# Where a block's second norm is applied: gathering x1 instead of h2, and transposing with a scaled diagonal

## The chip, the cores and the metric

The kernel runs on one core of a Trainium2 chip. TensorE (PE in the profile, PEld for its weight loads), VectorE (DVE), ScalarE (ACT) and GpSimd (POOL) compute; SyncE (SP) issues most DMAs, and POOL the indirect ones. The metric is the device time of one launch in microseconds (us).

## The reference

One decoder block of 1024 tokens with 1024 features, all in float32. After two kinds of attention and an out-projection comes a mixture of 32 experts, of which each token uses two:

```python
x  = x + gate_mix * (mixed @ w_out)                       # x1 in the kernel
h2 = rmsnorm(x, g_ffn) * (1 + scale_ffn) + shift_ffn
group  = argmax(softmax(h2 @ w_group))                    # 4 groups of 8 experts
top_p, expert = top_k(softmax(h2 @ w_expert within group), 2)
weight = max(group softmax) * top_p / sum(top_p)
y[token] += weight * ((silu(h2 @ w_gate[e]) * (h2 @ w_up[e])) @ w_down[e])
out = rmsnorm(x + gate_ffn * y, g_final)
```

Scale, shift and gates come from a conditioning vector, one value per feature. So h2 of a token is x1 times one factor of the token (r2, the reciprocal root of its mean square), times one factor per feature (`affn`), plus one shift per feature.

## The kernel before

The program goes through projections, eight attention passes, an out-projection with routing, the experts, and a last norm. Instructions stand in program order on each engine; the order of what lies beside attention is written out in lists of units (`work`, `end_units`), which are taken a few at a time between the steps of a pass.

The weights of the experts come in 384 loads of 512 KB, twelve per expert (eight for gate and up, four for down), through one SP queue (`load_to`, L973). Each load goes into a slot of the pool `u`, which has 49 slots that all large tiles share: a slot is 128 partitions by 1028 floats (4112 bytes; 4128 from slot to slot in the compiled program), of which most tiles use 1024. Some 36 loads are issued ahead; from the 35th on they are queued behind the gather of expert 1 (`after`).

In the last attention pass and after it, each 128-token tile goes through units: `out_mm` makes x1 (L674); `norm2` squares it on ACT and stores it to `acc` in DRAM; `norm2r` makes r2 on POOL (L933 and the helper `rsqrt`, L177 to L193); `norm2b` makes h2 from x1 in place, a DVE multiply by r2 and a feature row (L940) and an addition of another feature row on POOL (L941; on DVE where `late`), and stores it to `h2d`; `route0` transposes x1, `logits` multiplies it by the router's matrix (the norm's feature factors are folded into that), `route1` picks group and experts in some twelve DVE steps, `exps` is on ACT, `route2` counts ranks, `lists` makes one list of token numbers per expert by a product of two one-hot matrices (L868, L869), and `route3` makes the weights (L876 to L882). Weights and expert numbers go in 16 bytes behind each row of `h2d`, so a row there has 4112 bytes. The last two tiles t and u are routed together, their DVE steps interleaved.

Then come a spread of the gate row (L626), 80 warm-up products (L268), the first gathers (`load_x`, an indirect DMA of up to 96 or 64 rows by POOL, L1226), and `places`, which sorts the experts from 4 on by size, so that their lists and weights are taken in that order (`perm`, `permi`, `lsP`).

The expert loop takes the steps of `order`: G is one of eight gate-and-up steps, X the transpose of the expert after the next (`xpose`, L1241, between the sixth and seventh G step of the expert before it), T transposes the activations, D is one of four down steps, Y weighs and adds to `acc` with an indirect DMA. `xpose` turns the gathered rows by eight TensorE transposes into one or two PSUM banks, copies these to SBUF on ACT (L1242), and makes the expert's weights `wt` from the 16 bytes (L1244, L1246).

Of the kernel before, what the change touches and what calls it, by code (L numbers as in the profile page):

```python
# [28 lines left out]
ROW = 1028  # L29
# [34 lines left out]
HS = 7  # L64
QS = "ASS"
# [4 lines left out]
RG = 1  # L70
# [32 lines left out]
def build(nc, tc, I, out, cap=CAP):  # L103
# [14 lines left out]
    QA, QH, QE = (E_[c] for c in QS)  # L118
# [16 lines left out]
    def slot(name, dt=F32):  # L135
        return up.tile([128, ROW], dt, name=name, tag="u")[:, :1024]

# [188 lines left out]
    rows = dp.tile([3, 1024], F32, name="rows")  # L326

    def ada_units():
        us = []
        st = {}  # L330

        def fetch(v, k):
            st[v, k] = ada(v, k)

        def red(v, k):
            ada_red(st[v, k], v, k)

# [21 lines left out]
        us.append(router)  # L359
        return us  # L360
# [383 lines left out]
    h2d = dp.tile([T, ROW], F32, name="h2d")  # L744
# [4 lines left out]
    perm = cp.tile([128, NE], F32, name="perm")  # L749
# [15 lines left out]
    def section(tt):  # L765

        if "room" not in R:
            R["room"] = slot("room")
        n = 320 * (TL.index(tt) % 3)
        return R["room"][:, n:n + 320]  # L770
# [21 lines left out]
    def route1(tt):  # L792
# [5 lines left out]
        V.scalar_tensor_tensor(zz[:, 0:36], lp, R2[tt], zc, op0=ALU.mult, op1=ALU.add)  # L798
# [40 lines left out]
    def route2(tt, before=()):  # L839
# [10 lines left out]
        j1, r["j"] = at[:, 256:256 + NE], at[:, 288:288 + NE]  # L850
# [13 lines left out]
    def lists(*tts):  # L864
        lp = bank(f"ls{tts[0]}", (cap, NE))
        ms = [(R[tt]["at"][c], R[tt][o]) for tt in tts for c, o in enumerate(("o1", "o2"))]
        for n, (a, o) in enumerate(ms):
            PE.matmul(lp, a, o, start=(n == 0), stop=(n == len(ms) - 1))  # L868
        V.tensor_add(ls if TL[-1] in tts else lacc, lacc, lp)  # L869

    def route3(tt):
# [10 lines left out]
        V.tensor_sub(ext[:, 2:3], ext[:, 0:1], ext[:, 1:2])  # L882
        QE.dma_start(h2d[tt * 128:tt * 128 + 128, 1024:ROW], ext[:, 1:5])
# [7 lines left out]
    def places():  # L891
# [13 lines left out]
        A.activation(lsT, c2[:32, 0:cap], AF.Copy)  # L905
# [13 lines left out]
    R2 = {}  # L919

    def norm2(tt):
        x1 = X1[tt]
        R[tt] = slot(f"x1T_{tt}")
        ss2 = R2[tt] = sp.tile([128, 2], F32, name=f"ss2_{tt}", tag="ss2")
# [3 lines left out]
        QA.dma_start(acc[tt * 128:tt * 128 + 128, :], x1)  # L928

    def norm2r(tt):  # L930
        ss2 = R2[tt]
        R2[tt] = sp.tile([128, 1], F32, name=f"r2_{tt}", tag="r2", bufs=3)
        (G if RG else V).tensor_add(ss2[:, 0:1], ss2[:, 0:1], ss2[:, 1:2])  # L933
        rsqrt(R2[tt], ss2[:, 0:1], 1, 1.0 / D, G if RG else V)
# [52 lines left out]
    def alloc_x(e):  # L987
        XE[e] = up.tile([128, ROW], F32, name=f"xe{e}", tag="u")
        G.memset(XE[e][:capof(e)], 0.0)

    def end_units():
# [3 lines left out]
        us = [p0(lambda: (load_bc(1, "a"), load_bc(2, "sh"), load_x1(TL[0], acc), load_x1(TL[1], acc)))]  # L995
# [9 lines left out]
        for n in range(KT + 1):  # L1005
# [216 lines left out]
    def load_x(e):  # L1222
        if e not in XE:
            alloc_x(e)
        xe = XE[e]
        g = G.indirect_dma_start(out=xe[:capof(e)], out_offset=None, in_=h2d[:],  # L1226
# [198 lines left out]
    with tc.If(rv > 0):  # L1425
# [15 lines left out]
        with tc.For_i(0, NE, 1) as e:  # L1441
# [6 lines left out]
            for tt in range(KT):  # L1448
                c = slice(tt * 128, tt * 128 + 128)
                x, xt, act, y, a = work2[tt % 2]  # L1450
                nc.sync.dma_start(x, h2d[c, 0:1024])
                for s in (0, 1):
                    tp = bank(f"oxp{tt}_{s}")
                    for i in range(4):
                        k = 4 * s + i
                        PE.transpose(tp[:, i * 128:(i + 1) * 128], x[:, k * 128:(k + 1) * 128], ident)
                    V.tensor_copy(xt[:, s * 512:(s + 1) * 512], tp)
# [109 lines left out]
```

## Time and profile before

| | us |
|---|---|
| median of three runs (lowest, highest) | 1358.26 (1356.75, 1359.79) |
| the profiled execution | 1359.39 |
| its span | 1357.5 |
| TensorE busy | 1173.9 (86%) |
| VectorE busy | 740.4 (55%) |
| ScalarE busy | 457.9 (34%) |
| GpSimd busy | 287.8 (21%) |

The times in the rows are those of the profiled execution, counted from the start of its span. A busy share over the whole span is a mean over stages with different limits, so the table is only the start: the rows below are cut by stage. A row of the timeline has its start, its duration, engine, line, operation, what is written from what, shapes, and in brackets how long the engine had been idle before and what released it. An fp32 product counts two records there.

### The profile page before, as it was taken

How to read it: one execution, taken by the hardware profiler on the slowest of the kernel's cores; microseconds unless marked ns; L12 is line 12 of the kernel's file. 1: busy time of each engine (PE TensorE's matmuls, PEld its weight loads, DVE VectorE, ACT ScalarE, POOL GpSimd, SP SyncE). 2: the span in 40 equal slices, each digit the busy share in tenths (PEclk: the TensorE clock that was granted, in tenths of full speed). 3: DMA queues.
4: the chain of work that ended last, by engine and by line, in shares of the span. 5: the costliest groups of instructions: out<-in, count | busy, mean ns of one | idle time of the engine just before them, and what ended most of it. 6: DMA issues, size and time to landing. Idle time of an engine off the chain costs nothing. (4 is left out here: it accounts for less than half of the span.)

```text
span 1357.5 us, 19273 instructions
## 1 busy us (share of the span) xinstructions
PE 1173.9 (86%) x6843; PEld 688.0 (51%) x6843; DVE 740.4 (55%) x1378; ACT 457.9 (34%) x913; POOL 287.8 (21%) x341
## 2 busy tenths in 40 slices
PE   4699989999999998898876999999998888888960
PEld 3487778778867885676655533333332222222310
DVE  6958773774697768788967233333332223322224
ACT  5246553655555445334322121111211111111112
POOL 3600100120000102325334121211221111111203
PEclk9799999999999999899988899999999999999995
DMA  9322432462101011457666889999999999999984
GB/s 355 152 78 93 162 133 94 144 53 69 32 16 47 17 63 40 151 183 264 217 217 233 282 314 374 355 360 363 365 371 369 362 368 370 373 373 378 347 279 190
DMA packets 92904, 305.65 MB, mean 225 GB/s; under 512 B 15681, under 2 KB 18113, under 8 KB 92802
## 3 DMA queue, kind: packets, MB, share of 16 engines
q1 hardware_dynamic: 85298, 283.08, 58.3%
q0 software_dynamic: 6352, 17.08, 5.4%
q10 hardware_dynamic: 1152, 4.19, 0.8%
q8 instruction: 56, 0.92, 0.3%
q14 instruction: 46, 0.38, 0.1%
HBM read 279.39 MB, written 29.65 MB: 228 GB/s over the span
## 5 line engine op out<-in xcount | busy, mean ns | idle before, releaser
L1255 PE MATMUL gu<-ew,xs 128*64 128x512 f32 x1024 | 249.8, 611 | 8.3 <-DMA ew<-we 8.0
L1313 DVE TENSOR_TENSOR ys<-y,bc_gate 64x512 f32<-64x512 f32 x64 | 44.0, 688 | 260.1 <-PE y L1262 109.4
L1255 PE MATMUL y<-ew,at 128*64 128x512 f32 x512 | 128.4, 620 | 25.6 <-DMA ew<-we 23.9
L1255 PEld LDWEIGHTS gu<-ew,xs 128*64 128x64 f32 x1024 | 63.7, 137 | 142.7 <-issue 88.5
L1328 POOL DMA_INDIRECT acc<-ys,lsP x27 | 38.9, 1440 | 361.7 <-DVE ys L1319 210.1
L555 PE MATMUL tp<-ident,P 128*128 128x128 f32 x576 | 89.0, 280 | 19.6 <-DVE P L539 8.0
L538 DVE TENSOR_TENSOR_SCAN K<-K 128x1024 f32<-128x1024 f32 (+7 forms) x64 | 94.1, 1470 | 5.9 <-ACT K L526 5.7
L1255 PEld LDWEIGHTS y<-ew,at 128*64 128x64 f32 x512 | 33.3, 138 | 113.0 <-DMA ew<-we 59.4
L579 PE MATMUL o<-PT,v 128*64 128x256 f32 (+1 forms) x640 | 78.3, 385 | 13.5 <-DVE PT L560 10.4
L555 PEld LDWEIGHTS tp<-ident,P 128*128 128x128 f32 x576 | 65.9, 142 | 38.4 <-issue 9.6
L522 ACT ACTIVATE P<-P,st 128x1024 f32<-128x1024 f32 (+7 forms) x64 | 49.8, 778 | 91.6 <-DVE st L520 47.8
L579 PEld LDWEIGHTS o<-PT,v 128*64 128x64 f32 x640 | 46.8, 145 | 45.3 <-DVE PT L560 13.0
L215 DVE CUSTOM_DVE_ANT_0 wada<-wada,sc 128x1024 f32<-128x1024 f32 x48 | 64.4, 1354 | 9.2 <-DMA wada<-w_adaT 9.1
L1262 PE MATMUL gu<-ew,xs 128*32 128x512 f32 x576 | 69.3, 598 | 0.0
L520 DVE CUSTOM_DVE_ANT_0 P<-S,B 128x1024 f32<-128x1024 f32 (+7 forms) x64 | 48.3, 756 | 35.6 <-PE S L507 31.1
L526 ACT ACTIVATE K<-S 128x1024 f32<-128x1024 f32 (+7 forms) x64 | 41.8, 654 | 72.8 <-PE S L509 33.6
L1281 DVE TENSOR_TENSOR act<-sg,gu 64x512 f32<-64x512 f32 x32 | 22.1, 690 | 78.0 <-ACT sg L1280 77.5
L1242 ACT ACTIVATE xs<-xp 128x384 f32<-128x384 f32 (+1 forms) x50 | 24.1, 518 | 110.9 <-PE xp L1241 54.9
L558 ACT ACTIVATE PT<-tp 128x512 f32<-128x512 f32 (+3 forms) x120 | 56.0, 494 | 15.8 <-PE tp L555 15.0
L1267 ACT ACTIVATE yt<-y 64x512 f32<-64x512 f32 x18 | 10.7, 593 | 147.2 <-PE xp L1241 115.1
L539 DVE TENSOR_TENSOR P<-P,K 128x1023 f32<-128x1023 f32 (+7 forms) x64 | 53.7, 838 | 5.7 <-ACT P L527 0.7
L1297 ACT ACTIVATE at<-ap 128x384 f32<-128x384 f32 (+1 forms) x32 | 14.2, 444 | 106.1 <-PE ap L1295 100.5
(634 smaller groups left out, 2576.0 us busy)
## 6 DMA issues: line engine op xcount, KB each, us to landing
ew<-we SPq DMA_DIRECT2D x384, 512.0 KB, 12.1
wada<-w_adaT SPq DMA_DIRECT2D x48, 512.0 KB, 5.9
wqk<-wqk SPq DMA_DIRECT2D x16, 512.0 KB, 3.6
xT<-xT SPq DMA_DIRECT2D x16, 256.0 KB, 5.3
wv<-wv SPq DMA_DIRECT2D x8, 512.0 KB, 7.3
B<-bias SPq DMA_DIRECT2D x8, 512.0 KB, 6.1
wo<-w_out SPq DMA_DIRECT2D x8, 512.0 KB, 4.7
x<-x SPq DMA_DIRECT2D x8, 512.0 KB, 4.3
```

The costliest lines, as they stand in the source:

```text
L215: V.tensor_tensor_reduce(w, w, sc, op0=ALU.mult, op1=ALU.add, scale=1.0, scalar=0.0, accum_out=modc[:, v * 8 + k:v * 8 + k + 1])
L520: V.tensor_tensor_reduce(e, s, Bt[p, hd][:, :L], op0=ALU.add, op1=ALU.min, scale=-0.125, scalar=BIG, accum_out=st[:, 0:1])
L522: A.activation(e, e, AF.Exp, bias=st[:, 0:1], scale=-1.0, accum_out=st[:, 2:3])
L526: A.activation(k[:, :L], s, AF.Sigmoid, scale=-0.125)
L538: V.tensor_tensor_scan(k[:, :L], k[:, :L], k[:, :L], 1.0, op0=ALU.mult, op1=ALU.bypass)
L539: V.tensor_mul(b[:, 1:L], b[:, 1:L], k[:, 0:L - 1])
L555: PE.transpose(tp[:, jl - 4 * x, :], e[:, (jl - qo) * 128:(jl - qo) * 128 + 128], ident)
L558: A.activation(dst, tp[:, j0 - 4 * x:j1 - 4 * x, :], AF.Copy)
L579: PE.matmul(ps[hd * 64:hd * 64 + 64, 0:w], VV[p][:, j, hd * 64:hd * 64 + 64], pt[hd][jl // 4][:, jl % 4, 0:w], start=(n == 0), stop=(n == ...
L1255: PE.matmul(ps[h * 64:h * 64 + 64, 0:512], a[:, i, 0:64], w[:, h * 512:h * 512 + 512], start=(i == 0), stop=(i == n - 1))
L1262: PE.matmul(ps[r:r + 32, 512:1024], a[:, j, 64:96], w[:, h * 512:h * 512 + 512], start=(j < 2), stop=(j >= n - 2))
L1313: V.tensor_mul(ys[0:64, n], ps[r, 0:512], g[r, n])
```

## The change

Tiles store x1 itself to DRAM (`x1d`, rows of 1024 floats, 4096 bytes) and the experts gather x1; h2 is nowhere formed in rows. `norm2b` goes, with its two feature rows and their slots, and x1 is stored in `norm2`, right behind its last step. In `xpose` the eight transposes become products with a diagonal matrix that holds r2 of the gathered tokens, and the eight results are copied to SBUF with the feature's factor and shift, in turn on ACT and DVE (`affine`). r2 and the routing weight reach the expert through the lists: the product in `lists` has 96 columns per expert list row in place of 32 (token, weight, r2), for which each tile makes six [128x32] products on DVE. `places` sorts all three. r2 of the last tile is made on DVE. The 16-byte rows go.

The last two tiles are routed one behind the other, u first. The three buffers of the gathers are taken once and cleared once (before the tail), where they were taken and cleared for each expert. The slots of the pool are 1024 floats, 4096 bytes, and the pool is placed first, behind a pad of 128 bytes.

```diff
+    pool("pad", 1).tile([128, 32], F32, name="pad")
+    up = pool("u", NSLOT)
     cp = pool("const", 1)
-    up = pool("u", NSLOT)
...
     def slot(name, dt=F32):
-        return up.tile([128, ROW], dt, name=name, tag="u")[:, :1024]
+        return up.tile([128, D], dt, name=name, tag="u")
...
-    h2d = dp.tile([T, ROW], F32, name="h2d")
+    x1d = dp.tile([T, D], F32, name="x1d")
...
         for c in (0, 1):
-            V.tensor_scalar(at[c], iot[:, 0:cap], rk[:, c:c + 1], tid[:, tt:tt + 1], op0=ALU.is_equal, op1=ALU.mult)
-        r["at"], r["rk"] = at, rk
+            V.tensor_scalar(at[c], iot[:, 0:cap], rk[:, c:c + 1], None, op0=ALU.is_equal)
+        yield
+        for c in (0, 1):
+            o = (o1, o2)[c]
+            V.tensor_scalar(ow[c][:, 0:NE], o, tid[:, tt:tt + 1], None, op0=ALU.mult)
+            V.tensor_scalar(ow[c][:, 2 * NE:3 * NE], o, r2A[:, tt:tt + 1], None, op0=ALU.mult)
+        r["at"] = at
...
-        V.tensor_sub(ext[:, 2:3], ext[:, 0:1], ext[:, 1:2])
-        QE.dma_start(h2d[tt * 128:tt * 128 + 128, 1024:ROW], ext[:, 1:5])
+        for c in (0, 1):
+            V.tensor_scalar(r["ow"][c][:, NE:2 * NE], r[("o1", "o2")[c]], ext[:, c:c + 1], None, op0=ALU.mult)
...
-        PE.transpose(c2[:32, 0:cap], lsf, ident[:cap, :cap])
+        for i in range(3):
+            PE.transpose(c2[:32, i * cap:i * cap + cap], lacc[:, i * NE:i * NE + NE], ident[:cap, :cap])
...
     def norm2(tt):
...
+        QH.dma_start(x1d[c, :], x1)
...
-    def norm2b(tt, late=False):
-        c = slice(tt * 128, tt * 128 + 128)
-        x1 = X1.pop(tt)
-        h2 = slot(f"h2_{tt}") if tt in TL[HS:] else x1
-        V.scalar_tensor_tensor(h2, x1, R2[tt], bc["a"], op0=ALU.mult, op1=ALU.mult)
-        (V if late else G).tensor_add(h2, h2, bc["sh"])
-        QH.dma_start(h2d[c, 0:1024], h2)
+        eng = V if tt == TL[-1] else G
+        eng.tensor_add(ss2[:, 0:1], ss2[:, 0:1], ss2[:, 1:2])
+        rsqrt(r2A[:, tt:tt + 1], ss2[:, 0:1], 1, 1.0 / D, eng)
...
-                    lambda: route0(t), lambda: norm2r(t), lambda: logits(t), lambda: lists(w),
-                    lambda: norm2b(t, LT0),
-                    lambda: run(route3(w), route1(u), route1(t)), lambda: (exps(u), exps(t)),
-                    lambda: run(route2(u), route2(t, [u])), lambda: run(route3(u), route3(t)),
-                    lambda: lists(u, t), lambda: [alloc_x(e) for e in range(3)], lambda: (count(u), count(t)))]
+                    lambda: route0(t), lambda: run(route1(u), route3(w)), lambda: exps(u), lambda: logits(t),
+                    lambda: norm2r(t), lambda: (run(route2(u)), count(u)), lambda: run(route3(u)),
+                    lambda: run(route1(t)), lambda: exps(t), lambda: lists(w, u),
+                    lambda: run(route2(t)), lambda: run(route3(t)), lambda: lists(t), lambda: count(t))]
+                us.insert(mark, p0(alloc_x))
...
+    def affine(k, dst, src):
+        if k % 2:
+            V.tensor_scalar(dst, src, affn[:, k:k + 1], modc[:, 24 + k:25 + k], op0=ALU.mult, op1=ALU.add)
+        else:
+            A.activation(dst, src, AF.Identity, scale=affn[:, k:k + 1], bias=modc[:, 24 + k:25 + k])
...
+        dg = xs[:c, 1024 - c:1024]
+        V.tensor_scalar(dg, ident[:c, :c], wl[:c, NE + i:NE + i + 1], None, op0=ALU.mult)
         n = 512 // c // 4 * 4
         for k0 in range(0, KT, n):
             tp = bank(f"xp{e}_{k0}", (128, n, c))
             for k in range(k0, k0 + n):
-                PE.transpose(tp[:, k - k0, :], xe[:c, k * 128:(k + 1) * 128], ident[:c, :c])
-            A.activation(st["x"][:, k0:k0 + n], tp, AF.Copy)
+                PE.matmul(tp[:, k - k0, :], xe[:c, k * 128:(k + 1) * 128], dg, start=True, stop=True)
+            for k in range(k0, k0 + n):
+                affine(k, st["x"][:, k], tp[:, k - k0, :])
```

## Rows read from the trace of the kernel before

**Rows 1.** Busy time per engine by stage: window, length, engines, PEclk, DMA share, GB/s.
```profile
613.00:702.00 89.00, 73.52 (x429) 55.89 (x430) 78.39 (x194) 35.59 (x78) 36.78 (x59) 0.97 0.66 229
...
730.00:761.00 31.00, 16.76 (x158) 15.30 (x156) 18.66 (x90) 5.31 (x18) 14.86 (x20) 0.72 0.64 216
761.00:796.00 35.00, 34.81 (x196) 10.42 (x196) 8.20 (x17) 8.24 (x15) 3.47 (x3) 0.95 0.88 316
800.00:1290.00 490.00, 446.62 (x2482) 135.46 (x2478) 153.22 (x250) 79.25 (x148) 99.97 (x92) 0.99 1.02 367
```

**Rows 2.** What SP's queue waits for, 761 to 796 us, then 800 to 1290 us.
```profile
SPq L973 <- PE gu L1262: 14.3, 5, 4.8
...
SPq L973 <- DMA ew<-we: 281.9, 280, 6.3
```

**Rows 3.** DMA issues between 800 and 1290 us: count, KB each, us to landing.
```profile
ew<-we SPq DMA_DIRECT2D x311, 512.0 KB, 12.6
```

**Rows 4.** Groups by line and shape, 613 to 702 us: busy us, mean ns, idle before.
```profile
L940 DVE SCALAR_TENSOR_TENSOR x<-x,r,bc_a 128x1024 f32<-128x1024 f32 x5 | 6.4, 1277 | 0.0
...
L941 POOL TENSOR_TENSOR x<-x,bc_sh 128x1024 f32<-128x1024 f32 x5 | 12.4, 2485 | 27.6 <-issue 11.9 <-PE op L671 7.3 <-PE tp L555 5.2
```

**Rows 5.** Timeline around 630 us, one POOL addition and two DVE scans.
```profile
630.46 2.94 POOL L941 TENSOR_TENSOR x<-x,bc_sh 128x1024 f32<-128x1024 f32 x1 [5.17 <-PE tp L555]
...
631.57 3.18 DVE L538 TENSOR_TENSOR_SCAN K<-K 128x640 f32<-128x640 f32 x1
...
636.64 1.48 DVE L538 TENSOR_TENSOR_SCAN K<-K 128x640 f32<-128x640 f32 x1
```

**Rows 6.** What TensorE waits for, 613 to 710 us: total us, times, longest.
```profile
PE o L579 <- DVE PT L560: 6.8, 3, 3.6
```

**Rows 7.** Timeline of the tail, 728 to 762 us.
```profile
729.39 0.74 DVE L674 SCALAR_TENSOR_TENSOR x<-op,r_out,x 128x512 f32<-128x512 f32 x1
...
736.86 1.28 DVE L940 SCALAR_TENSOR_TENSOR h<-x,r,bc_a 128x1024 f32<-128x1024 f32 x1 [2.34 <-POOL r L184]
...
738.13 0.41 DVE L798 SCALAR_TENSOR_TENSOR zz<-lg,r,zc 128x36 f32<-128x36 f32 x2
738.29 2.34 POOL L941 TENSOR_TENSOR h<-h,bc_sh 128x1024 f32<-128x1024 f32 x1 [1.47 <-DVE den L876]
...
738.66 1.98 DVE L880 TENSOR_TENSOR extA<-extA,e 128x1 f32<-128x1 f32 x1
...
740.57 2.74 POOL L989 MEMSET xe<- 96x1028 f32 x3
...
741.09 2.26 DVE L808 TENSOR_SCALAR pen<-iot,igf 128x4 f32<-128x4 f32 x2
...
745.25 0.23 DVE L827 TENSOR_SCALAR room<-iot,extA 128x32 f32<-128x32 f32 x1
...
748.11 0.18 DVE L869 TENSOR_TENSOR ls<-lacc,ls 96x32 int32<-96x32 f32 x1
...
760.07 0.88 PE L1241 MATMUL xp<-ident,xe 96*128 96x96 f32 x8
```

**Rows 8.** Timeline of TensorE, three xpose steps in a row.
```profile
823.47 0.88 PE L1241 MATMUL xp<-ident,xe 96*128 96x96 f32 x8
...
841.22 0.70 PE L1241 MATMUL xp<-ident,xe 64*128 64x64 f32 x8
...
871.85 0.71 PE L1241 MATMUL xp<-ident,xe 64*128 64x64 f32 x8
```

**Rows 9.** Timeline of TensorE around 729 us, eight products and eight transposes.
```profile
728.23 1.94 PE L787 MATMUL lt<-x1T,wr 128*36 128x128 f32 x16
...
730.17 1.07 PE L780 MATMUL x1p<-ident,x 128*128 128x128 f32 x8
```

**Rows 10.** Timeline of SP, three weight loads issued in a row.
```profile
1233.76 0.33 SPq L973 DMA_DIRECT2D ew<-we  x1
1234.99 0.33 SPq L973 DMA_DIRECT2D ew<-we  x1
1236.26 0.33 SPq L973 DMA_DIRECT2D ew<-we  x1
```

More of the change, by code (lines that the diff above doesn't have):

```diff
@@ L28 @@
 NSLOT = 49
-ROW = 1028
 BIG = 1.0e30
@@ L69 @@
 LT = 0
-RG = 1
 NT = 0
@@ L117, in build @@
     E_ = dict(S=nc.sync, A=A, G=G, V=V)
-    QA, QH, QE = (E_[c] for c in QS)
+    QA, QH = (E_[c] for c in QS)
     GATE = [0]
@@ L325, in build @@
     acc = dp.tile([T, D], F32, name="acc")
-    rows = dp.tile([3, 1024], F32, name="rows")
+    rows = dp.tile([1, 1024], F32, name="rows")
     def ada_units():
@@ L344, in fin @@
             V.scalar_tensor_tensor(affn, modc[:, 32:40], 1.0, g_ffn, op0=ALU.add, op1=ALU.mult)
-            for i, src in enumerate((modc[:, 16:24], affn, modc[:, 24:32])):
-                nc.sync.dma_start(rows[i].rearrange("(k p) -> p k", p=128), src)
+            nc.sync.dma_start(rows[0].rearrange("(k p) -> p k", p=128), modc[:, 16:24])
         def router():
@@ L752, in build @@
     capx = cp.tile([32, 128], F32, name="capx")
-    lacc = cp.tile([cap, NE], F32, name="lacc")
+    lacc = cp.tile([cap, 3 * NE], F32, name="lacc")
     ls = cp.tile([cap, NE], I32, name="ls")
+    wlP = cp.tile([cap, 2 * NE], F32, name="wlP")
+    r2A = cp.tile([128, KT], F32, name="r2A")
     zzs = [cp.tile([128, 40], F32, name=f"zz_{i}") for i in (0, 1)]
     G.memset(csum, 0.0)
-    G.memset(lacc, EMPTY)
+    G.memset(lacc[:, 0:NE], EMPTY)
+    G.memset(lacc[:, NE:3 * NE], 0.0)
     for t8 in zzs:
@@ L765, in section @@
     def section(tt):
[L767 to L770, printed above, removed]
+        i = TL.index(tt) % 3
+        if ("room", i // 2) not in R:
+            R["room", i // 2] = slot(f"room{i // 2}")
+        return R["room", i // 2][:, i % 2 * 512:i % 2 * 512 + 512]
     def route0(tt):
@@ L775, in route0 @@
         x1T = R[tt]
+        X1.pop(tt)
         for x in (0, 1):
@@ L849, in route2 @@
         at = section(tt)
-        j1, r["j"] = at[:, 256:256 + NE], at[:, 288:288 + NE]
+        j1 = at[:, 256:256 + NE]
+        r["ow"] = ow = [at[:, c:c + 3 * NE] for c in (288, 384)]
         at = [at[:, c * 96:c * 96 + cap] for c in (0, 1)]
@@ L864, in lists @@
     def lists(*tts):
-        lp = bank(f"ls{tts[0]}", (cap, NE))
-        ms = [(R[tt]["at"][c], R[tt][o]) for tt in tts for c, o in enumerate(("o1", "o2"))]
+        lp = bank(f"ls{tts[0]}", (cap, 3 * NE))
+        ms = [(R[tt]["at"][c], R[tt]["ow"][c]) for tt in tts for c in (0, 1)]
         for n, (a, o) in enumerate(ms):
             PE.matmul(lp, a, o, start=(n == 0), stop=(n == len(ms) - 1))
-        V.tensor_add(ls if TL[-1] in tts else lacc, lacc, lp)
+        if TL[-1] in tts:
+            V.tensor_add(ls, lacc[:, 0:NE], lp[:, 0:NE])
+        V.tensor_add(lacc, lacc, lp)
     def route3(tt):
@@ L910, in places @@
         PE.matmul(c3[:, 0:32], eb, pm, start=True, stop=True)
-        PE.matmul(c3[:cap, 32:64], lsT, pm, start=True, stop=True)
+        for i in range(3):
+            PE.matmul(c3[:cap, 32 + 32 * i:64 + 32 * i], lsT[:, i * cap:i * cap + cap], pm, start=True, stop=True)
         V.tensor_copy(permi, c3[0:1, 0:32])
-        V.tensor_copy(perm, c3[:, 0:32])
         V.tensor_copy(lsP, c3[:cap, 32:64])
+        V.tensor_copy(wlP, c3[:cap, 64:128])
         V.tensor_scalar(cp_, rank, float(len(SMALL)), float(cap - CAPS), op0=ALU.is_ge, op1=ALU.mult)
         V.tensor_scalar(capx, ones[:32], cp_, float(CAPS), op0=ALU.mult, op1=ALU.add)
-    R2 = {}
+    SS2 = {}
     def norm2(tt):
+        c = slice(tt * 128, tt * 128 + 128)
         x1 = X1[tt]
         R[tt] = slot(f"x1T_{tt}")
-        ss2 = R2[tt] = sp.tile([128, 2], F32, name=f"ss2_{tt}", tag="ss2")
+        ss2 = SS2[tt] = sp.tile([128, 2], F32, name=f"ss2_{tt}", tag="ss2")
+        QH.dma_start(x1d[c, :], x1)
         for h in (0, 1):
@@ L927, in norm2 @@
             A.activation(R[tt][:, n], x1[:, n], AF.Square, accum_out=ss2[:, h:h + 1])
[L928 removed]
+        QA.dma_start(acc[c, :], x1)
     def norm2r(tt):
[L931 to L934, printed above, removed]
[L936 to L942 removed]
+        ss2 = SS2.pop(tt)
+        eng = V if tt == TL[-1] else G
+        eng.tensor_add(ss2[:, 0:1], ss2[:, 0:1], ss2[:, 1:2])
+        rsqrt(r2A[:, tt:tt + 1], ss2[:, 0:1], 1, 1.0 / D, eng)
     EW, XE, ST, EREG = {}, {}, {}, {}
@@ L985, in load_to, with alloc_x @@
             loaded[0] += 1
-    def alloc_x(e):
-        XE[e] = up.tile([128, ROW], F32, name=f"xe{e}", tag="u")
-        G.memset(XE[e][:capof(e)], 0.0)
+    def alloc_x():
+        for e in range(3):
+            XE[e] = slot(f"xe{e}")
+            G.memset(XE[e][:cap], 0.0)
     def end_units():
         p0 = lambda f: (f, 0, None)
-        us = [p0(lambda: (load_bc(1, "a"), load_bc(2, "sh"), load_x1(TL[0], acc), load_x1(TL[1], acc)))]
+        us = [p0(lambda: (load_x1(TL[0], acc), load_x1(TL[1], acc)))]
         def spread(us, mark, to):
@@ L1013, in end_units @@
                 us.append((lambda t=TL[n]: out_mm(1, t, 0), 2, rdy))
-            if XN == 1 and 1 < n + 1 < KT:
+            if 1 < n + 1 < KT:
                 us.append(p0(lambda t=TL[n + 1]: load_x1(t, acc)))
             if n < KT:
-                put(lists, 3)
                 put(lambda t: run(route3(t)), 3)
-            if n + 2 < KT and not XN:
-                us.append(p0(lambda t=TL[n + 2]: load_x1(t, acc)))
-            if n < KT:
                 put(lambda t: run(route1(t)), 2)
@@ L1026, in end_units @@
                 put(lambda t: (out_mm(1, t, 1), norm2(t)), 0, 2)
-                if XN == 2 and n + 2 < KT:
-                    us.append(p0(lambda t=TL[n + 2]: load_x1(t, acc)))
                 put(logits, 1, 1)
+                put(lists, 3)
                 put(lambda t: (run(route2(t)), count(t)), 2)
-                put(lambda t, n=n: norm2b(t, n >= LATE), 1)
             else:
@@ L1222, in load_x @@
     def load_x(e):
[L1223 to L1226, printed above, removed]
+        g = G.indirect_dma_start(out=XE[e % 3][:capof(e)], out_offset=None, in_=x1d[:],
                                  in_offset=bass.IndirectOffsetOnAxis(ap=listof(e), axis=0),
@@ L1230, in load_x @@
             after[0] = g.ins
-    def xpose(e):
-        xe, c = XE.pop(e), capof(e)
-        st = ST[e] = {}
-        st["x"] = slot(f"xs{e}")[:, :KT * c].rearrange("p (k t) -> p k t", k=KT)
+    def affine(k, dst, src):
[3 more added lines that the diff above has]
+            A.activation(dst, src, AF.Identity, scale=affn[:, k:k + 1], bias=modc[:, 24 + k:25 + k])
+    def xpose(e):
+        xe, c = XE[e % 3], capof(e)
+        wl, i = (lacc[:, NE:3 * NE], e) if e < NF else (wlP, e)
+        xs = slot(f"xs{e}")
+        st = ST[e] = dict(wt=wl[:c, i:i + 1], x=xs[:, :KT * c].rearrange("p (k t) -> p k t", k=KT))
+        dg = xs[:c, 1024 - c:1024]
+        V.tensor_scalar(dg, ident[:c, :c], wl[:c, NE + i:NE + i + 1], None, op0=ALU.mult)
         n = 512 // c // 4 * 4
@@ L1450, in build @@
                 x, xt, act, y, a = work2[tt % 2]
-                nc.sync.dma_start(x, h2d[c, 0:1024])
+                nc.sync.dma_start(x, x1d[c, :])
+                dg = y[:, 0:128]
+                V.tensor_scalar(dg, ident, r2A[:, tt:tt + 1], None, op0=ALU.mult)
                 for s in (0, 1):
                     tp = bank(f"oxp{tt}_{s}")
[L1454 to L1457, printed above, removed]
+                    for k in range(4 * s, 4 * s + 4):
+                        PE.matmul(tp[:, k % 4 * 128:k % 4 * 128 + 128], x[:, k * 128:(k + 1) * 128], dg,
+                                  start=True, stop=True)
+                    for k in range(4 * s, 4 * s + 4):
+                        affine(k, xt[:, k * 128:(k + 1) * 128], tp[:, k % 4 * 128:k % 4 * 128 + 128])
                 ps = wide(f"ogu{tt}")
```

22 lines of the change are left out of this document (6 added, 16 removed).

## The prediction

> **What bounds the kernel now.** I read the page's 40 slices first: DVE's digits are 8 and 9 around the middle of the span, the DMAs' are 9 in all of the last third. Where these stretches begin and end I took from the timeline, and the table of windows gives each stage its own busy times [rows 1]. From 613 to 702 us (last attention pass, with out-projection and routing beside it) DVE works 78.39 of 89.00 us. From 730 to 761 us, the routing tail, no engine passes 18.66 of 31.00: a chain of small dependent steps. From 761 to 796 us TensorE is full, 34.81 of 35.00, while the DMAs move 316 GB/s. From 800 to 1290 us the DMAs are full: share 1.02, 367 GB/s, TensorE 446.62 of 490.00. The waits say which of the two comes first. SP, which issues the weight loads, waits from 761 to 796 us for TensorE to release a slot (14.3 us at one line), and from 800 to 1290 us for its own earlier loads (281.9 us in 280 waits) [rows 2]. So the start of the expert loop is TensorE's, the rest belongs to the DMAs: 311 loads in 490 us, 490 / 311 = 1.576 us each [rows 3].
>
> **Attention pass.** norm2b goes. On DVE that is its multiply, 1.277 us, five times before the pass ends: 6.4 us [rows 4]. Its addition of 2.485 us on POOL goes too, five times, and it had slowed DVE: a scan of 128x640 took 3.18 us beside it and 1.48 without it [rows 5]; 1.7 here, some 1.4 us each by my estimate, 7 us. Added are six [128x32] operations a tile; one such takes 0.23 us alone and less in a row of them, since they overlap [rows 7]: I take 1.0 a tile, less a small subtraction that goes, 4.4 us in five tiles. DVE thus gains 6.4 + 7 - 4.4 = 9.0 at most. The end is set by the last PV products, and TensorE was held for DVE's copies PT only 6.8 us in this stretch, in three waits of which the longest is 3.6 [rows 6]. I take -5.5, between 0 (TensorE then waits for the next thing, say the scan) and -9. x1 is stored from SP right after its second half; the h2 store that it replaces stood in the same queue, so no load waits longer.
>
> **Tail, up to the lists.** From the last x1 (729.39) to `ls` (748.11) are 18.7 us [rows 7]. Gone: DVE's wait of 2.34 us for POOL's factor, norm2b's multiply 1.28, its POOL addition, beside which a 1-element multiply took 1.98, and a [128x4] operation of 2.26 beside POOL's memsets, both about 0.2 when undisturbed: 1.8 + 2.0 us. That is 7.4 us. Added: twelve list operations of the last two tiles, 0.2 each, 2.4 us (six more fall on the third-last tile's weights and the larger addition: 0.4); the factor on DVE, thirteen one-element steps (at 0.23 each 3.0; they are shorter, I take 1.9); and u and t one behind the other: the interleaved pair took from 738.13 to 745.48, 7.3 us, 2.0 of them in the step of 2.26, so 5.3 undisturbed. One alone has twelve steps of some 0.23, 2.8, twice that 5.5, and a second passage to TensorE and ACT and back costs perhaps 2.0: +2.2. Sum -7.4 + 6.9 = -0.5; bounds -4 (if DVE fills u's steps into t's waits) and +3 (if the memsets, which the change puts early, fall on DVE's steps again). The store of the 16-byte rows before the first gather goes too; TensorE's first transpose comes after the warm-up products and `places`, not after that gather alone, so I count nothing, and -1 as the end.
>
> **Places and the first transpose.** Three transposes and three list products in place of one (about 0.15 each, +0.6) and a copy three times as wide (+0.1). DVE's diagonal of the first expert stands in program order behind five copies and compares of `places` that in the kernel before run on beside the first transposes (these start at 760.07 [rows 7]): +1.0 less what the copies overlap. The eight evictions alternate on two engines, four of some 0.25 us each, against two wide ones of some 0.45: 0. Sum +1.6 (0.5 to 3). So TensorE starts the experts 4.4 us earlier: -5.5 - 0.5 + 1.6.
>
> **Four first experts, where TensorE paces.** One xpose takes 0.88 us and the period is 17.75 us [rows 8]. The products with the diagonal are plain fp32 products. A row for the price: 8 products of 128x128 are 16 records and 1.94 us, 8 transposes are 8 records and 1.07 [rows 9]. By that ratio the new xpose costs +0.8 us. The nearest bounds are 0 and +2.4 (four times). Three xe slots are held for good, where two or three lived before: some one slot less for loads, one load of 1.58 us at worst; I take 1.0. That would be 3.2 + 1.0 if every later release made a load later; the DMAs' share of 0.88 [rows 1] leaves them room to make some of it up, and I take half: +2.0. Bounds 0 and +10 (four times 2.4).
> The Trainium skill, TensorE: Matmul & The Clock Gate, section Terms, calls transposes four times as fast as fp32 products. By that rule this term would be +10 and the sum below about -4; the two rows show a factor of 1.8.
>
> **The long stretch.** TensorE's work per expert grows by 0.8 us there too, DVE's by one diagonal and four evictions, some 1.2 us, of an engine busy 153 of 490 us [rows 1]. TensorE on its own needs 30.6 us for a pair of one large and one small expert (the transposes from 841.22 to 871.85 [rows 8]), 15.3 each, and the DMAs bring an expert's 12 loads in 18.9: 3.6 us each cover it. What changes the pace is where a slot lies. Slots were 1028 floats wide and the program lays them 4128 bytes apart, so one in eight begins on a multiple of 256 bytes. The change makes them 4096 bytes, behind a pad that is put first, so that all begin so. Where nothing else moves, SP issues a load each time an earlier one lands, and the step is 1.27 us, and 1.23 where the load that landed went into a slot on such a multiple [rows 10]. I take 0.037 us a load, for seven in eight of some 290 loads (the first of the 311 fall where TensorE still sets the pace): -9.3. Bounds: 0 (the rows are few, and gathers and adds share the time) and -13 (0.045, a hundredth more a load, for nearly all 311).
> The Trainium skill, DMA: Bandwidth & Descriptors, section How a descriptor splits into AXI transactions, says that a descriptor that starts off a 256-byte boundary fetches from the boundary below, and the unused bytes cost beats of 32. For 4096 bytes that is one to seven beats on 128, an estimate of 0.04 us on average, and about -10 for the term. The trace agrees in size; that the price grows with the offset its rows don't show.
> The gathered rows shrink from 4112 to 4096 bytes in the gathers there, and no small rows are stored beside them: -0.5, by 0.4% of their share, from 0 to -5.
>
> **Sum.** -5.5 - 0.5 + 1.6 + 2.0 - 9.3 - 0.5 = -12.2 us. It is made against the profiled execution, 1359.39 us, of which the span is 1357.5 and 1.9 lie around it; that gives 1347.2. The median of the runs is 1358.26, 1.1 below it, so the forecast is 1346.
>
> **Rivals.**
> 1. The slot addresses do nothing for the pace (the step of 1.23 is chance). For it: two steps are little. Against it: the loads of that stretch are alike in all else. The -9.3 goes: -2.9, 1355.
> 2. Attention does not end earlier, since what holds TensorE there is the scan chain itself, while the slots work: the -5.5 goes, -6.7 and 1351.5. For it: the scan takes most of DVE's time. Against it: DVE is at 88% and loses five long operations.
> 3. Slower: xpose makes TensorE the bound in the long stretch. Place: the products between two gate-and-up products, in each of 26 experts. With the quicker loads the DMAs need 18.9 - 0.4 = 18.5 us an expert, so it decides from 3.2 us more in each xpose. Price: at four times the transposes' 0.8 us it is +2.4; with eight evictions that hold TensorE's banks, in turn on two engines and behind what these have to do, 1.2 more, +3.6. The long stretch then loses 0.4 x 26 = 10 us, and the first four experts 4 x (3.6 - 0.8) = 11: -12.2 + 21 = +9, 1367. For it: the next products stand behind the transposes on TensorE's one queue, and the transposes now wait for DVE too. Against it: the two rows of the ratio, and that xs is needed only two products before the next expert begins.
> 4. The change doesn't relieve DVE as it says: its small operations cost more in the pass than norm2b did (0.25 us each, and no slowing by POOL beside the long ones), and the pass ends 2 us later: -12.2 + 7.5 = -4.7, 1353.5.
>
> **Chances.** Forecast 0.55; rival 1, 0.22; rival 2, 0.09; rival 4, 0.06; rival 3, 0.08. The forecast's own range is 1339 to 1352. The range of 8 in 10 adds rivals 1, 2 and 4: 1336 to 1357. 0.2% is 2.7 us, about what can be told from no change: slower has rival 3 and the far end of rival 1, 0.09; same takes part of rival 1, whose time is 1355 with its own spread of some 4 us, 0.09; faster the rest, 0.82.
>
> **What would show it.** Steps of SP at about 1.23 where nothing else moves, and 1.54 us per load over the long stretch. The last PV products about 5 us earlier, `ls` at about 18 us after the last x1. xpose as 16 records of about 1.6 us and a period near 18.5 us for the first experts. The forecast is wrong in kind if TensorE's idle time in the long stretch falls to nothing, or if the loads there keep 1.27.

## The result and the profile after

The changed kernel takes 1479.15 us (median; usual runs 1473.33 to 1481.6) against 1357.51 before: ratio 1.0889, 95% interval [1.0848, 1.0929]. It is slower by 121.6 us, where 1346 and 0.82 for faster were forecast. Its first profiled execution (1850.38 us) had a granted clock of 0.637 throughout, unlike the timed runs (0.91 to 0.92), so the rows below are from a second profile of the same file (run e1_again, span 1471.2 us, clock 0.92).

The table of windows of the changed kernel, with the columns of [rows 1]:

```profile
761.00:796.00 35.00, 31.36 (x178) 11.37 (x168) 10.27 (x18) 7.06 (x14) 2.50 (x2) 0.90 0.80 270
800.00:1290.00 490.00, 421.62 (x2154) 164.79 (x2152) 141.50 (x272) 85.88 (x177) 55.57 (x46) 0.89 0.88 315
```

The long stretch was full in the DMAs before, share 1.02 and 367 GB/s, with a clock of 0.99. Now the DMAs stand at 0.88 and 315 GB/s, TensorE at 421.62 of 490, and its clock at 0.89. Neither is full, so something makes both wait. What TensorE waits for, 750 to 1400 us (total us, times, longest):

```profile
PE xp L1245 <- DVE xs L1240: 73.6, 30, 3.6
PE ap L1296 <- DVE act L1288: 14.2, 13, 1.2
```

L1240 is the diagonal. In all but two of the experts xpose finds it missing. The timeline of one such place shows why (start, duration, engine, line, operation):

```profile
772.20 1.92 PE L1263 MATMUL y<-ew,at 128*32 128x512 f32 x16
...
774.05 1.08 PE L1256 MATMUL gu<-ew,xs 128*64 128x512 f32 x4
774.21 1.39 DVE L1314 TENSOR_TENSOR ys<-y,bc_gate 64x512 f32<-64x512 f32 x2 [7.69 <-PE y L1263]
775.70 0.59 ACT L1268 ACTIVATE yt<-y 64x512 f32<-64x512 f32 x1 [7.35 <-DVE ys L1314]
776.32 0.68 DVE L1269 TENSOR_TENSOR yt<-yt,y 64x512 f32<-64x512 f32 x1 [0.72 <-ACT yt L1268]
777.04 1.38 DVE L1320 TENSOR_TENSOR ys<-yt,bc_gate 32x512 f32<-32x512 f32 x2
778.45 0.27 DVE L1240 TENSOR_SCALAR xs<-ident,lacc 96x96 f32<-96x96 f32 x1
...
778.77 3.73 PE L1245 MATMUL xp<-xs,xe 96*128 96x96 f32 x16 [3.64 <-DVE xs L1240]
```

The diagonal takes 0.27 us and needs only the lists, which have been there since the routing. But it is written into DVE's program after Y of the expert two before (L1314, L1269, L1320), and Y's first operation waits for that expert's last down product, which ends at 774.1. Until then DVE had been idle for 7.69 us and could not pass it. From the end of the product to the diagonal's end are 4.6 us; TensorE has one gate-and-up step of 1.08 us ahead of xpose to fill them, and idles 3.64. Behind an expert of 64 rows Y has only the first pair of operations, and the wait is 0.91 us.

The wait is not the whole price. A later xpose with the products behind it, and then the windows of 3 us around it (the granted clock is the third number from the end):

```profile
1004.46 3.73 PE L1245 MATMUL xp<-xs,xe 96*128 96x96 f32 x16 [3.64 <-DVE xs L1240]
1008.12 7.83 PE L1256 MATMUL gu<-ew,xs 128*64 128x512 f32 x24
```

```profile
998.00:1001.00 3.00, 2.82 (x20) 0.50 (x19) 1.10 (x2) 0.00 (x0) 0.00 (x0) 1.00 1.03 422
1001.00:1004.00 3.00, 0.00 (x0) 0.00 (x0) 2.21 (x4) 0.59 (x1) 0.00 (x0) 0.81 1.02 415
1004.00:1007.00 3.00, 2.54 (x12) 2.54 (x13) 0.39 (x3) 0.43 (x1) 2.30 (x2) 0.50 1.02 416
1007.00:1010.00 3.00, 3.00 (x12) 1.60 (x13) 1.50 (x4) 1.29 (x3) 0.14 (x1) 0.50 0.84 227
1010.00:1013.00 3.00, 3.00 (x10) 0.83 (x8) 0.53 (x1) 0.59 (x1) 0.00 (x0) 0.50 0.36 81
1013.00:1016.00 3.00, 3.00 (x18) 0.83 (x18) 0.64 (x2) 0.00 (x0) 0.00 (x0) 0.98 0.96 352
```

TensorE stood still from 1000.8 to 1004.46, the clock fell from 1.00 to 0.50 (1.2 of 2.4 GHz), and it was back only after 1013. In that time the 16 records of xpose (8 products) take 3.73 us and the 24 gate-and-up records behind it 7.83, where at full clock they take 2.02 and 5.37 (e5, below). Only the place at 1216 us is as dear: behind the other late xposes of 96, wherever 24 such records stand in a row, they take 6.58 to 6.92.

### The profile page after: what moved, and what is told of

Same layout as the page of the kernel before. It is cut to its first block, busy times and chain, and to the rows that moved or that the text cites. A ratio compares the mean times of both kernels' runs of the same rounds, so it can differ in the third digit from the quotient of the medians.

```text
span 1848.6 us, 19966 instructions
## 1 busy us (share of the span) xinstructions
PE 1692.2 (92%) x7104; PEld 896.3 (48%) x7104; DVE 753.0 (41%) x1515; ACT 496.5 (27%) x991; POOL 237.4 (13%) x296
## 4 chain that ended last, share of the span: by engine, by line
PE 86%; DVE 9%; DMA 1%; ACT 1%; POOL 1%; issue 1%; SPq 0%; ACTq 0%; POOLq 0%; DVEq 0%
PE gu L1256 17%; PE y L1256 9%; PE xp L1245 6%; PE gu L1263 5%; PE o L573 5%; PE tp L549 5%; PE pj L418 4%; PE pj L417 4%; PE pj L419 4%; PE y L1263 3%; PE S L500 3%; PE S L501 3%; PE op L663 2%; PE op L664 2%; PE op L665 2%; DVE ys L1314 2%
## 5 line engine op out<-in xcount | busy, mean ns | idle before, releaser
L1256 PE MATMUL gu<-ew,xs 128*64 128x512 f32 x1024 | 376.7, 884 | 0.0
L1314 DVE TENSOR_TENSOR ys<-y,bc_gate 64x512 f32<-64x512 f32 x64 | 44.0, 687 | 378.6 <-PE y L1263 203.7
L1256 PEld LDWEIGHTS gu<-ew,xs 128*64 128x64 f32 x1024 | 80.4, 168 | 214.3 <-issue 204.2
L1256 PE MATMUL y<-ew,at 128*64 128x512 f32 x512 | 174.3, 848 | 0.5 <-ACT at L1298 0.5
L1245 PE MATMUL xp<-xs,xe 96*128 96x96 f32 (+1 forms) x512 | 104.4, 378 | 61.4 <-DVE xs L1240 60.3
L1245 PEld LDWEIGHTS xp<-xs,xe 96*128 96x128 f32 (+1 forms) x512 | 98.0, 293 | 102.9 <-DVE xs L1240 100.4
L1231 ACT ACTIVATE xs<-xp,modc,affn 128x96 f32<-128x96 f32 (+1 forms) x128 | 53.7, 420 | 272.3 <-PE xp L1245 238.9
L549 PE MATMUL tp<-ident,P 128*128 128x128 f32 x576 | 116.6, 345 | 5.6 <-DVE P L533 5.1
L1229 DVE TENSOR_SCALAR xs<-xp,affn,modc 128x96 f32<-128x96 f32 (+1 forms) x128 | 46.4, 362 | 146.8 <-ACT xs L1231 146.8
L573 PE MATMUL o<-PT,v 128*64 128x256 f32 (+1 forms) x640 | 102.0, 479 | 3.9 <-DVE PT L554 3.9
L1263 PE MATMUL gu<-ew,xs 128*32 128x512 f32 x576 | 102.2, 852 | 0.0
```

Source lines behind the costliest of these rows:

```text
L549: PE.transpose(tp[:, jl - 4 * x, :], e[:, (jl - qo) * 128:(jl - qo) * 128 + 128], ident)
L573: PE.matmul(ps[hd * 64:hd * 64 + 64, 0:w], VV[p][:, j, hd * 64:hd * 64 + 64], pt[hd][jl // 4][:, jl % 4, 0:w], start=(n == 0), stop=(n == ...
L1245: PE.matmul(tp[:, k - k0, :], xe[:c, k * 128:(k + 1) * 128], dg, start=True, stop=True)
L1256: PE.matmul(ps[h * 64:h * 64 + 64, 0:512], a[:, i, 0:64], w[:, h * 512:h * 512 + 512], start=(i == 0), stop=(i == n - 1))
L1263: PE.matmul(ps[r:r + 32, 512:1024], a[:, j, 64:96], w[:, h * 512:h * 512 + 512], start=(j < 2), stop=(j >= n - 2))
L1314: V.tensor_mul(ys[0:64, n], ps[r, 0:512], g[r, n])
```

## The experiments

**The changed kernel again, for the profile.** No edit.

> The changed kernel itself once more, for a profile at the clock of its usual runs (some 1479 us). Theory A (each xpose waits for its diagonal, which stands on DVE behind the weighting of the expert before): TensorE's waits for L1240 sum to 60 us or more over the experts, 2.5 to 4 us behind each expert of 96, and the granted clock falls below the 0.99 of before in the same stretch. Rival B (the products with the diagonal and the eight evictions are what costs): those waits are under 30 us in sum, and the xpose rows themselves are 2 us or more longer than before.

1473.75 us, ratio 1.0848 [1.0819, 1.0877]. Waits for the diagonal 73.6 us in 30 places, up to 3.6; clock 0.89. Both as theory A has it. But rival B's rows are there too: xpose at 3.73 us in place of 0.88. The next run tells how much of that is the clock.

**The diagonal an expert ahead.**

```diff
-        dg = xs[:c, 1024 - c:1024]
-        V.tensor_scalar(dg, ident[:c, :c], wl[:c, NE + i:NE + i + 1], None, op0=ALU.mult)
+        if e not in DG:
+            diagonal(e)
+        dg = DG.pop(e)
...
+        if e + 1 < NE:
+            diagonal(e + 1)
```

`diagonal` makes it with the same operation in a buffer of its own (two in turn), at the end of the xpose before.

> Only the diagonal moves: that of the next expert is made at the end of each xpose, in a buffer of its own, so that it is ready an expert ahead. Theory A: the wait and the lower clock go, and with them nearly the whole loss: 1340 to 1360 us. Rival B: the products and evictions stay, 1420 us or more. Between the two, both cost.

1341.02 us (1335.94 to 1344.85), ratio 0.9859 [0.9827, 0.989]: 132.7 us less than e1_again on the same chip, and faster than before. So nearly the whole loss comes from where the diagonal is made. Groups of TensorE by line and shape, 740 to 1420 us (busy us, mean ns | idle before), first of e1_again:

```profile
L1256 PE MATMUL gu<-ew,xs 128*64 128x512 f32 x1004 | 273.7, 676 | 0.0
...
L1245 PE MATMUL xp<-xs,xe 96*128 96x96 f32 x288 | 64.6, 416 | 59.3 <-DVE xs L1240 58.2 <-issue 1.1
...
L1245 PE MATMUL xp<-xs,xe 64*128 64x64 f32 x224 | 29.6, 285 | 15.5 <-DVE xs L1240 15.5
```

and of e2_diag_ahead:

```profile
L1268 PE MATMUL gu<-ew,xs 128*64 128x512 f32 x1024 | 248.9, 612 | 1.7 <-DMA ew<-we 1.6
...
L1255 PE MATMUL xp<-dg,xe 96*128 96x96 f32 x288 | 38.1, 288 | 1.1 <-issue 1.1
...
L1255 PE MATMUL xp<-dg,xe 64*128 64x64 f32 x224 | 29.6, 285 | 0.0
```

The waits (58.2 + 15.5 = 73.7 us) are gone; xpose of 96 loses 26.5 us and the gate-and-up products 24.8, by the same work at full clock. 73.7 + 26.5 + 24.8 = 125 of the 128.1 us between the two spans (1471.2 and 1343.1). Twenty records of the first group are missing in e1_again, so its part is a little larger. The xpose of 64 keeps its 285 ns in both, behind waits of 0.91 us; but behind five of these thirteen waits the next eight gate-and-up records take 2.95 to 3.30 us where the others take 1.94, so a wait of 0.91 us sometimes costs clock too, and part of the 24.8 is theirs.

**Filling the wait.** The changed kernel with work for TensorE in front of the late xposes:

```diff
         elif kind == "X":
+            if capof(e) > 64 and e > 1:
+                warm(11)
             xpose(e)
```

`warm(11)` issues 44 bf16 products of 128x128 into a scratch bank.

> The changed kernel, with 44 small bf16 products (as in the warm-up) issued in front of each xpose of an expert of 96 from expert 2 on, so that TensorE works while the diagonal is late. If the loss is two things, the wait itself (73.6 us in the profile) and the lower clock behind it (some 26 us in the xpose rows, 25 in the gate-and-up rows): the waits are filled, the clock stays near 0.99 and the time falls by 40 to 55 us, to about 1425. If the clock has nothing to do with the waits: no gain, 1474 or more.

1438.61 us (1437.88 to 1445.59), ratio 1.0619 [1.0585, 1.0653]: 35 us less than e1_again by medians, 31 by the ratios, with work added and the diagonal as late as before. The direction is as expected, the size a little under it. Groups of e5_filler, same columns:

```profile
L1256 PE MATMUL gu<-ew,xs 128*64 128x512 f32 x1024 | 270.9, 659 | 0.0
...
L263 PE MATMUL scr<-onesb 128*128 128x128 bf16 x704 | 42.1, 219 | 0.0
L1245 PE MATMUL xp<-xs,xe 96*128 96x96 f32 x288 | 38.1, 288 | 18.3 <-DVE xs L1240 17.2 <-issue 1.1
```

The xposes of 96 are back at 38.1 us, so their extra 26.5 was the clock alone. The idle time before xposes fell from 74.8 us (59.3 + 15.5) to 34.3 (18.3, and 16.0 before those of 64), with 42.1 us of filler in its place; where the filler stands, 1.08 us of waiting are left. The clock of the stretch from 800 to 1290 us is 0.96, for 0.89 without the filler. The gate-and-up products came back in part only (270.9, for 248.9 in e2). One place is a wait that was not filled (3.61 us, an expert of 64 at 847 us, clock 0.50 behind it). Nearly all others, but for one at 778 us, stand behind short waits from 1098 us on:

```profile
1023.30 2.02 PE L1245 MATMUL xp<-xs,xe 96*128 96x96 f32 x16 [1.07 <-DVE xs L1240]
1025.25 5.37 PE L1256 MATMUL gu<-ew,xs 128*64 128x512 f32 x24
...
1098.66 2.02 PE L1245 MATMUL xp<-xs,xe 96*128 96x96 f32 x16 [1.07 <-DVE xs L1240]
1100.61 7.07 PE L1256 MATMUL gu<-ew,xs 128*64 128x512 f32 x24
```

The six xposes of 96 between 872 and 1061 us are all like the first pair, and between 1000 and 1045 us the clock is 1.00 in every 3 us; the seven from 1098 us on are like the second, with a clock of 0.66 and 0.77 in the 6 us behind 1100. The products behind the unfilled 0.96 us of the experts of 64 change at the same time: eight records take 1.94 us up to 1081 us, and 2.8 to 3.6 after that. Why the same wait costs clock only there is not shown.

**Another place for xpose.** One number of the changed kernel, which puts X behind T and ahead of the down steps, and so ahead of Y:

```diff
-XA, TA, DA = 6, 4, 5
+XA, TA, DA = 4, 4, 5
```

> The changed kernel with one number changed (XA 6 to 4): xpose of the expert after the next then stands behind T and ahead of the down steps, so its diagonal is ahead of Y's weighting on DVE. If the place of the diagonal behind that weighting is the cause: like e2, 1336 to 1350, with no wait over 1 us for the diagonal. If any place of it on DVE costs (the activations' operations stand ahead of it here): waits of 1 us and more remain, and 1360 or over.

1342.76 us (1340.25 to 1346.1), ratio 0.9896 [0.9864, 0.9927]. No wait for a diagonal is left in its table of waits. Here the diagonal keeps its buffer and its place in xpose, so it is neither the buffer, which e2 changed too, nor the diagonal on DVE as such, but what stands in front of it, and one number is enough to mend it.

**Transposes in place of products.** No diagonal, r2 left out of the gathered tokens:

```diff
-                PE.matmul(tp[:, k - k0, :], xe[:c, k * 128:(k + 1) * 128], dg, start=True, stop=True)
+                PE.transpose(tp[:, k - k0, :], xe[:c, k * 128:(k + 1) * 128], ident[:c, :c])
```

> xpose uses the identity and eight transposes as before, with no diagonal (r2 is left out of the gathered tokens); the evictions with factor and shift stay. Theory A: like e2, within 10 us of it, 1335 to 1360. Rival B in the products: well below e2. Rival C (something else in the change, say the order of the tail or the xe slots held for good): still over 1420.

1336.34 us (1333.82 to 1337.02), ratio 0.9832 [0.9809, 0.9854], 4.7 us under e2 by medians, with overlapping intervals: products with the diagonal cost no more than about that at the end, though each xpose is more than 1 us longer. Rival C is out.

**r2 by ACT.** The whole result, with transposes, and the gathered rows scaled in place:

```diff
+        A.activation(xe[:c], xe[:c], AF.Copy, scale=wl[:c, NE + i:NE + i + 1])
```

This stands for expert e + 2 behind the transpose of the activations of expert e.

> The changed kernel with r2 put on the gathered rows in place by ACT (one 96x1024 or 64x1024 operation, some 1 us, an expert and more ahead, while ACT waits for the down steps), and eight transposes with the identity in place of the products with the diagonal. If the products cost what e3 shows (5 us under e2) and ACT's operation is hidden: 1334 to 1340, the fastest whole kernel. If ACT's operation delays the activations: 1341 or more.

1336.82 us (1333.92 to 1338.41), ratio 0.9853 [0.9826, 0.9879]. As expected by time; its ratio can't be told from e2's 0.9859. Both beat the kernel before and the changed one.

**Where the slots begin.** e2 with a pad of 160 bytes, then of 352, in place of 128 (the pools placed behind the slots move with them):

```diff
-    pool("pad", 1).tile([128, 32], F32, name="pad")
+    pool("pad", 1).tile([128, 40], F32, name="pad")
```

> e2 with a pad of 160 bytes in place of 128, so that every slot begins 32 bytes behind a multiple of 256. If the address sets the pace of the loads as predicted: 8 to 12 us more than e2, and steps of SP near 1.27 us where e2 has 1.23. If not: e2's time within 2 us.

> e2 with every slot 224 bytes behind a multiple of 256, where e4 had 32. If the price is any start off the multiple: e4's 1352, within 3 us. If it grows with the unused bytes, by beats: seven times e4's, far over 1352 (1380 and more).

32 bytes off: 1352.31 us (1349.43 to 1357.26), ratio 0.9956 [0.9939, 0.9973], 11.3 us over e2 on the same chip. 224 bytes off: 1351.09, ratio 0.9966 [0.9948, 0.9984]. So the address costs 10 to 15 us (by medians and by ratios), and the same for one eighth as for seven eighths of the multiple. The steps of SP, where a row of two loads lasts one step and the 0.33 us of the second, of e2 and then of e4:

```profile
1206.33 1.57 SPq L974 DMA_DIRECT2D ew<-we  x2
```

```profile
1208.38 1.60 SPq L974 DMA_DIRECT2D ew<-we  x2
```

1.24 us against 1.27, as [rows 10] had it; two such rows of e7 give 1.28 and 1.30. The long stretch points the same way: 372 GB/s in e2 and 367 in e4 and e7 (800 to 1270 us). Over its 470 us that is some 6 us of the 10 to 15; where the rest arises was not followed. The same pad under e6:

> e6 with every slot 32 bytes off the multiple of 256. e6 has TensorE less full than e2, so the loads set its pace sooner: by e4 and e7 (10 to 11 us over e2) the difference to e6's 1337 should be 10 to 14 us. If the address costs only where TensorE and the loads are both full: under 6 us.

1344.69 us (1341.93 to 1347.56), ratio 0.9895 [0.9868, 0.9922]: 7.9 us over e6 by medians, 5.7 by the ratios. That is under the 10 to 14 expected, and by the ratios it is within the "under 6" of the other case. The sign is the same, but the two intervals overlap a little, and why the address should cost less where TensorE is less full, or whether that is noise, stays open.

**POOL beside the attention pass.** e2 with an unused addition where norm2b's stood:

```diff
+        G.tensor_add(slot(f"pd{tt}"), x1, x1)
```

It runs for six tiles and takes 1.89 us each, where norm2b's took 2.49 [rows 4].

> e2 with an addition of 128x1024 on POOL for six tiles, where the kernel before had norm2b's; its result is used by nothing. If a good half of what the attention pass gained is DVE freed from POOL: the last PV products start 5 to 8 us later than in e2 (689.5) and the time is 4 to 8 us more. If only the removed DVE multiply counts: within 2 us of e2.

1341.95 us (1340.6 to 1344.97), ratio 0.9886 [0.9864, 0.9909]. The place where it acts shows it: the last PV products before the pass, the last of the pass and the first xpose, first of e2, then of e8:

```profile
603.33 0.87 PE L573 MATMUL o<-PT,v 128*64 128x256 f32 x8
...
689.50 3.45 PE L573 MATMUL o<-PT,v 128*64 128x256 f32 x30 [0.69 <-DVE PT L554]
...
744.19 3.70 PE L1255 MATMUL xp<-dg,xe 96*128 96x96 f32 x16 [1.10 <-issue]
```

```profile
604.16 0.87 PE L573 MATMUL o<-PT,v 128*64 128x256 f32 x8
...
696.25 3.46 PE L573 MATMUL o<-PT,v 128*64 128x256 f32 x30 [0.69 <-DVE PT L554]
...
750.58 3.70 PE L1264 MATMUL xp<-dg,xe 96*128 96x96 f32 x16 [1.09 <-issue]
```

The last PV products start 6.75 us later and the xpose 6.4, but 0.83 us of that is there before the pass. The pass itself, from the first row to the second, takes 86.17 us in e2 and 92.09 in e8, 5.92 more; in the nine profiles with the pass of e2 it takes 84.6 to 87.2. DVE has 213 operations in it in both:

```profile
603.33:689.50 86.17, 76.95 (x453) 58.31 (x453) 72.21 (x213) 39.76 (x84) 25.65 (x56) 0.98 0.66 238
```

```profile
604.16:696.25 92.09, 80.47 (x454) 60.59 (x453) 78.91 (x213) 39.53 (x84) 34.82 (x61) 0.94 0.63 223
```

They take 6.7 us more beside the additions (78.91 for 72.21). DVE also waits 3.2 us for POOL's r2 in e8, so not all of the 5.92 need be slower operations. At the end of the kernel the expected 4 to 8 us do not show: the medians differ by 0.9 us, the ratios by 3.7 with overlapping intervals, the spans of the two profiles by 0.1. So the gain of DVE from POOL's silence is shown for the start of the experts, and how much of it reaches the end is not.

## Why the prediction was wrong, point by point

**The step that failed** stands in "The long stretch": DVE's work per expert "by one diagonal and four evictions, some 1.2 us, of an engine busy 153 of 490 us", covered by the loads' pace. I priced the diagonal by its duration and DVE's busy share. It is a wait added to TensorE, and what decides is what stands ahead of the diagonal in DVE's order: Y, whose first operation waits for TensorE itself. Rival 3 had the place (xpose), the side (slower) and even that "the transposes now wait for DVE too", but put 1.2 us on evictions and waits, and 0.08 on the whole; the measured extra of an xpose of 96 is 3.64 us of wait, 2.85 us of longer products (3.73 for 0.88) and 1.2 to 2.5 us in the products behind it, 8 to 9 us. What I held against it, that xs is not needed until two products later, is about who uses the result; TensorE is in order, so the xpose that waits holds these two products too. In "Places" I had even found the same diagonal queued behind DVE's operations, for the first expert alone.

**The clock.** No term of the forecast let it fall. The gaps of before in the long stretch [rows 1] left it at 0.99; those of 3.64 us took it to 0.50, for some 9 us at the place shown. Between e1 and e2 the lower clock cost 51 us (26.5 + 24.8), a part of it behind the waits of 0.91 us.

**Transposes and products.** By the rule of the Trainium skill that transposes are four times as fast as fp32 products (TensorE: Matmul & The Clock Gate, Terms), the xpose of 96 would take 3.5 us, as an estimate. At full clock it takes 2.02 for 0.88, a factor of 2.3; the one of 64 2.00 for 0.71, 2.8. The trace lies between that rule and the 1.8 of [rows 9].

In the sum I had taken +0.8 us for what is +1.14 and +1.29; the ratio of 1.8 would even have made it +0.7 on 0.88. The ratio was the wrong thing to carry over: 16 records of products took 1.94 us in [rows 9] and take 2.02 and 2.00 here, for 96 and 64 tokens alike, while eight transposes go from 1.07 to 0.88 and 0.71 as the tokens get fewer.

**The other terms**, read in e2, which differs from the changed kernel in the diagonal alone:
- Attention pass: forecast -5.5, at most -9. The last PV products went from 701.85 to 689.50, -12.35, but 5.3 of that lies ahead of the pass, where the PV products start at 608.63 before and at 603.33 in e2. It need not be the change's: in e3, with e2's program up to the experts, they start at 608.60. Before:

```profile
608.63 0.87 PE L579 MATMUL o<-PT,v 128*64 128x256 f32 x8
...
701.85 4.53 PE L579 MATMUL o<-PT,v 128*64 128x256 f32 x20 [2.06 <-DVE PT L560]
```

  The pass took 93.22 us there and 86.17 in e2: -7.05, between the forecast and the bound. DVE's work in it fell by 10.6 us (82.77 to 72.21), more than the 9.0 that I had as the most. e8 gives 5.92 of the 7.05 back, with POOL's additions and no multiply on DVE.
- Tail: forecast -0.5. From the last x1 to `ls` 15.85 us in place of 18.72, -2.9, within its bounds. The end points in e2:

```profile
715.55 0.74 DVE L668 SCALAR_TENSOR_TENSOR x<-op,r_out,x 128x512 f32<-128x512 f32 x1
...
731.40 0.18 DVE L874 TENSOR_TENSOR ls<-lacc,ls 96x32 int32<-96x32 f32 x1 [0.90 <-PE ls L872]
```

- Places: from `ls` to the first xpose 12.79 us for 11.96, and from its start to the first gate-and-up product 3.6 us for 1.1, the xpose itself 3.70 at a lower clock. Forecast +1.6 for both, at most +3, measured +3.3. The eight evictions, which I had as four of 0.25 us on each engine side by side, take 0.43 and 0.38 and follow each other (last section).
- First four experts: a period of 18.9 us for 17.75 [rows 8], +1.15 each, in e2:

```profile
794.03 2.02 PE L1255 MATMUL xp<-dg,xe 96*128 96x96 f32 x16
...
812.93 2.02 PE L1255 MATMUL xp<-dg,xe 96*128 96x96 f32 x16
...
1015.06 2.02 PE L1255 MATMUL xp<-dg,xe 96*128 96x96 f32 x16
...
1029.86 2.00 PE L1255 MATMUL xp<-dg,xe 64*128 64x64 f32 x16
...
1048.06 2.02 PE L1255 MATMUL xp<-dg,xe 96*128 96x96 f32 x16
```

  The two last rows of 96 are a pair of experts apart: 33.0 us where 30.6 were TensorE's pace before.
- Slot addresses: forecast -9.3 for seven slots in eight; e4 measures 11.3 for all, so 9.9. Right in sign and size; the steps of SP are the place, but the figures of the long stretch show only some 6 us of it. The Trainium skill's beats (DMA: Bandwidth & Descriptors, How a descriptor splits into AXI transactions) would make 224 bytes off dearer than 32, by seven beats to one; e4 and e7 show no difference.
- Sum without the failed step: 1346 forecast, 1341 with e2's edit. Part of that is compensation, and so luck: the first xpose starts 15.9 us earlier, 5.3 of them from ahead of the pass, where 4.4 were forecast for TensorE's start, and the products cost more.

## What to carry to other kernels

The new operation on a lightly used engine cost by what stood ahead of it in that engine's program and what that was waiting for, not by its 0.27 us or the busy share. Before it is made to feed another engine, write down the last instruction ahead of it and who releases that one; if it is the engine that will wait, the loop has an idle stretch, a bubble, in every turn. Operations whose inputs are long there belong a turn ahead. And a bubble on TensorE had a second price here, in the clock of the products behind it.

## What the runs showed of the hardware

The granted clock fell from 1.00 to 0.50 behind an idle time of 3.64 us and stayed there for about 9 us (e1, 1004 us). Idle times of about 1 us did this in some places and not in others: 1.07 us in front of e5's xposes left it at 1.00 around 1023 us and were followed by 0.66 and 0.77 behind 1100 us; of thirteen of 0.91 us in e1, five were followed by slower products. No run shows what decides.

ACT's and DVE's evictions of one xpose did not run beside each other: in e2 each waits for the one before (0.45 to 0.5 us of idle time). The eight of the first xpose took from 746.2 to 749.6 us; later ones, where DVE was at Y until 1018.4, from 1016.3 to 1020.9, and ended so:

```profile
1020.06 0.43 ACT L1231 ACTIVATE xs<-xp,modc,affn 128x96 f32<-128x96 f32 x1 [0.45 <-DVE xs L1229]
...
1020.52 0.38 DVE L1229 TENSOR_SCALAR xs<-xp,affn,modc 128x96 f32<-128x96 f32 x1 [0.50 <-ACT xs L1231]
```

A start of the slots 32 or 224 bytes off a multiple of 256 cost the kernel the same (1352.31 and 1351.09 us, for 1341.02), with steps of 1.27 and of 1.28 to 1.30 us a load in the rows read, for 1.24.
